# First projection on unscaled transposes, the row scale applied after the product

## The chip, the cores and the metric

The kernel runs on one core of a Trainium2 chip. The metric is the device time of one execution in microseconds (us); of several executions the median is given. Engines are named as in the profile: PE (TensorE, matrix products), DVE (VectorE), ACT (ScalarE), POOL (GpSimd), SP (SyncE, which issues most transfers).

## What is computed

Two transformer blocks on 256 rows of 2048 numbers, in float32. The change is in the first lines of the first block: a root-mean-square norm, and the projection `w_pw1` of a convolution module, whose output goes through a gate.

```python
def rms_norm(x, g):
    xf = x.astype(jnp.float32)
    y = xf * lax.rsqrt(jnp.mean(xf * xf, axis=-1, keepdims=True) + NORM_EPS)
    return (y * g.astype(jnp.float32)).astype(x.dtype)
...
def conformer_conv(h, w_pw1, b_pw1, w_dw, b_dw, ln_g, ln_b, w_pw2, b_pw2):
    u = h @ w_pw1 + b_pw1
    a, gate = jnp.split(u, 2, axis=-1)
    u = a * jax.nn.sigmoid(gate)
```

Behind it come a depthwise convolution over 31 rows, a layer norm, the projection `w_pw2`, a feed-forward part, and the second block with attention and another feed-forward part.

## The kernel before

**Split products.** Every float32 operand of a large product is split in two: `hi` is the operand rounded to the type that PE takes in one pass (`fp32r`), `lo` is the rest. A product is the sum of three, hi by hi, hi by lo and lo by hi. The weights are split as they arrive: ACT casts `raw` to `hi` (L127), DVE or POOL subtracts to get `lo` (L128). The activations are split the same way by `split_act` (L177: ACT casts, DVE subtracts).

**Steps.** The work is a list of steps, each with one weight tile (`unit_std` and its kind) and a function that issues its products. `emit` walks the list: it loads three tiles ahead (`LOADS`) and splits one tile ahead in the first three steps and two ahead later. All instructions are issued in the order in which the Python code runs, and each engine works through its own in that order. So where a line stands in `split` or in a step's function sets what waits behind it.

**The first projection.** `w_pw1` is worked in groups of 256 + 256 output columns (the value and its gate). A group has four steps, one for each quarter of the 2048 inputs; I call the step of group g and quarter c *unit (g, c)*. A unit is 4 column blocks by 4 input blocks by 3 products, 48 instructions on PE (L523, L525, L526), with tokens along the free axis (256 of them). The activations are transposed for that: tile `xa` c holds quarter c, hi and lo, and all groups read the same four tiles.

**The start, before.** x is loaded in four transfers of 512 KB (L253), and ACT sums the squares of all of it, eight times 512 columns (`sumsq`, L208). From the sums comes r = 1/rms for each row (`rstd_of`, L195). Only then ACT and DVE scale x by r (`first_a`, L298 and L300), PE transposes the scaled rows (L303), DVE multiplies by the norm's gain (`first_b`, L312), and `split_act` makes `xa`. The first product (L523) comes behind that.

**Behind a group.** After the last quarter `glu` (L348) applies the gate: ACT a sigmoid (L354), DVE a product that lands in PSUM (L358), ACT a copy (L360). `diags` (L363) makes diagonal matrices of the filter on ACT (L372), and `conv` (L383) runs 3 of 31 taps on PE (L391, tile `ca`) and the rest on DVE (L399). The conv of group 0 stands on PE behind unit (1, 0).

POOL splits the weights from tile 5 on in this part of the program (the kind "p" and i > 4 in `split`), and between tiles 6 and 7 it makes constants (L319 to L329).

## Time and profile before

| | |
|---|---|
| median of 3 runs | 2189.69 us (2189.35 to 2191.28) |
| the profiled execution | 2189.95 us, of which the profile's span is 2188.2 us |
| PE busy | 2151.5 us (98%) |
| DVE busy | 1439.0 us (66%) |
| ACT busy | 959.2 us (44%) |
| POOL busy | 175.2 us (8%) |
| transfers | 395.41 MB at a mean of 181 GB/s |

A row of a timeline gives start, length, engine, line, operation, the tiles (written<-read), the shapes and how many instructions were merged; in brackets stands how long the engine had been idle before, and what ended that. A row of the table by windows gives for each engine the busy time, and then PE's granted clock (1.00 is full), the busy share of the DMA engines, and GB/s.

### The profile page before, as it was taken

The numbers are of one execution on the slowest core, as the hardware profiler recorded it, in microseconds if no ns is written. First come the engines' busy times: TensorE is split into PE (matmuls) and PEld (weight loads), VectorE is DVE, ScalarE is ACT, GpSimd is POOL, SyncE is SP. The second block draws the span as 40 slices with busy tenths as digits, with TensorE's granted clock in tenths as the row PEclk, the third lists the DMA queues.
The fourth block names the chain that finished last, engine by engine and source line by source line (L and its number), as shares of the span: only waits on it lengthen the run. The fifth ranks groups of instructions, "written<-read, shape, count | busy, mean of one in ns | idle before, by whom it ended". The sixth has DMA issues, their size and how long they took to land.

```text
span 2188.2 us, 27599 instructions
## 1 busy us (share of the span) xinstructions
PE 2151.5 (98%) x11521; PEld 1862.8 (85%) x11521; DVE 1439.0 (66%) x1648; ACT 959.2 (44%) x965; POOL 175.2 (8%) x88
## 2 busy tenths in 40 slices
PE   7999899999999999999999999999999999999998
PEld 6999778888888888888788888888888888888886
DVE  5997775656665666566866565676656665666656
ACT  6454454434333433343545454454333433343333
POOL 2887500000000000000000000000000000000000
PEclk9999999999999999999999999999999999999999
DMA  7555255555655565556544554555565556555653
GB/s 228 164 165 148 74 184 192 189 192 178 202 193 192 178 205 192 189 179 221 177 161 154 176 170 154 162 185 181 192 204 191 178 190 203 189 182 195 196 190 133
DMA packets 219613, 395.41 MB, mean 181 GB/s; under 512 B 8994, under 2 KB 46018, under 8 KB 219074
## 3 DMA queue, kind: packets, MB, share of 16 engines
q1 hardware_dynamic: 216160, 389.05, 54.3%
q10 hardware_dynamic: 2960, 4.27, 0.6%
q8 instruction: 90, 1.47, 0.3%
q0 software_dynamic: 368, 0.34, 0.1%
q14 instruction: 35, 0.28, 0.0%
HBM read 391.53 MB, written 2.10 MB: 180 GB/s over the span
## 4 chain that ended last, share of the span: by engine, by line
PE 95%; DVE 2%; ACT 1%; issue 0%; DMA 0%; ACTq 0%; SPq 0%; DVEq 0%
PE up L219 21%; PE up L225 11%; PE dn L236 11%; PE dn L238 11%; PE dn L237 11%; PE pj L219 5%; PE pw L526 2%; PE pw L523 2%; PE pw L525 2%; PE pj L225 2%; PE ca L391 2%; PE wo L238 1%; PE wo L237 1%; PE wo L236 1%; PE pv L238 1%; PE pv L237 1%
## 5 line engine op out<-in xcount | busy, mean ns | idle before, releaser
L128 DVE TENSOR_TENSOR lo<-raw,hi 128x2048 fp32r<-128x2048 f32 (+1 forms) x339 | 774.3, 2284 | 511.1 <-ACT hi L127 510.8
L127 ACT CAST hi<-raw 128x2048 fp32r<-128x2048 f32 (+1 forms) x369 | 702.8, 1906 | 852.7 <-PE dn L238 320.1
L219 PE MATMUL up<-xn,hi 128*128 128x512 f32 x2048 | 482.3, 390 | 0.0
L219 PEld LDWEIGHTS up<-xn,hi 128*128 128x128 f32 x2048 | 380.2, 188 | 76.1
L236 PE MATMUL dn<-hi,act 128*128 128x512 f32 x1024 | 398.6, 389 | 0.0
L238 PE MATMUL dn<-hi,act 128*128 128x512 f32 x1024 | 398.4, 389 | 0.0
L237 PE MATMUL dn<-lo,act 128*128 128x512 f32 x1024 | 398.3, 389 | 0.0
L225 PEld LDWEIGHTS up<-xn,lo 128*128 128x128 f32 x2048 | 254.2, 192 | 5.0
L225 PE MATMUL up<-xn,lo 128*128 128x256 f32 x2048 | 255.7, 283 | 0.0
L646 DVE SCALAR_TENSOR_TENSOR res<-dn,rsq,res 128x512 f32<-128x512 f32 x256 | 191.3, 747 | 56.8 <-PE dn L238 56.8
L238 PEld LDWEIGHTS dn<-hi,act 128*128 128x128 f32 x1024 | 192.2, 188 | 40.0
L236 PEld LDWEIGHTS dn<-hi,act 128*128 128x128 f32 x1024 | 192.2, 188 | 39.8
L237 PEld LDWEIGHTS dn<-lo,act 128*128 128x128 f32 x1024 | 192.2, 188 | 39.8
L399 DVE SCALAR_TENSOR_TENSOR acc<-u_p,wd,acc 128x256 f32<-128x256 f32 x385 | 151.6, 474 | 0.0
L128 POOL TENSOR_TENSOR lo<-raw,hi 128x2048 fp32r<-128x2048 f32 x30 | 138.5, 4621 | 85.9 <-ACT hi L127 85.9
L523 PE MATMUL pw<-xa,hi 128*128 128x256 f32 x448 | 129.1, 288 | 0.7 <-ACT hi L127 0.7
L526 PE MATMUL pw<-xa,lo 128*128 128x256 f32 x448 | 127.6, 285 | 0.9 <-DVE lo L128 0.9
L525 PE MATMUL pw<-xa,hi 128*128 128x256 f32 x448 | 127.5, 285 | 0.0
L219 PE MATMUL pj<-xn,hi 128*128 128x512 f32 x512 | 122.4, 392 | 1.9 <-DVE q_t L911 1.9
L219 PEld LDWEIGHTS pj<-xn,hi 128*128 128x128 f32 x512 | 94.5, 188 | 21.8 <-DVE q_t L911 3.0
L631 ACT COPY u_t<-up 128x512 f32<-128x512 f32 x64 | 37.7, 589 | 159.6 <-PE up L219 159.6
L633 DVE TENSOR_TENSOR u_z<-up,u_t 128x512 f32<-128x512 f32 x64 | 44.3, 692 | 77.7 <-ACT u_t L631 77.7
(255 smaller groups left out, 2003.9 us busy)
## 6 DMA issues: line engine op xcount, KB each, us to landing
raw<-in_ffn_w_up_dram SPq DMA_DIRECT2D x64, 1024.0 KB, 5.1
raw<-in_ffn_w_down_dram SPq DMA_DIRECT2D x64, 1024.0 KB, 5.1
raw<-in_w_up_dram SPq DMA_DIRECT2D x64, 1024.0 KB, 5.1
raw<-in_w_down_dram SPq DMA_DIRECT2D x64, 1024.0 KB, 5.1
raw<-in_w_in_dram SPq DMA_DIRECT2D x48, 1024.0 KB, 5.0
raw<-in_conv_w_pw_dram SPq DMA_DIRECT2D x64, 512.0 KB, 4.8
raw<-in_conv_w_pw_dram SPq DMA_DIRECT2D x16, 1024.0 KB, 5.1
raw<-in_w_out_dram SPq DMA_DIRECT2D x16, 1024.0 KB, 5.0
```

Source lines behind the costliest of these rows:

```text
L127: nc.scalar.copy(hi[:, j:j + n], raw[:, j:j + n])
L128: e.tensor_tensor(out=lo[:, j:j + n], in0=raw[:, j:j + n], in1=hi[:, j:j + n].bitcast(F32), op=ALU.subtract)
L219: mm(ps[m], hi[:, k, m * P:(m + 1) * P], xt[:, k, :, :], start=(kq == 0 and k == 0), stop=(kq == 3 and k == 3), skip_group_check=True)
L225: mm(ps[m][:, 0:T], lo[:, k, m * P:(m + 1) * P], xt[:, k, 0, :], start=False, stop=False, skip_group_check=True)
L236: mm(ps[h], xh, hi[:, k, :], start=(first and k == 0), stop=False)
L237: mm(ps[h], xh, lo[:, k, :], start=False, stop=False)
L238: mm(ps[h], xl, hi[:, k, :], start=False, stop=(last and k == 3))
L399: nc.vector.scalar_tensor_tensor(out=acc[k], in0=src, scalar=w, in1=acc[k], op0=ALU.mult, op1=ALU.add)
L523: mm(ps[:, m, :], wh, xt[:, k, 0, :], start=first and m % 2 == 0, stop=False, skip_group_check=True)
L525: mm(ps[:, m, :], wh, xt[:, k, 1, :], start=False, stop=False, skip_group_check=True)
L526: mm(ps[:, m, :], wl, xt[:, k, 0, :], start=False, stop=last, skip_group_check=True)
L646: nc.vector.scalar_tensor_tensor(out=r, in0=ps[h], scalar=state["rsq"][:, h:h + 1], in1=r, op0=ALU.mult, op1=ALU.add)
```

## The change

It has five parts.

1. **Loads.** x now comes in eight transfers, by quarters of its columns, and the first three weight tiles are issued between the quarters. Weight tile 0 comes in four transfers (its two input halves apart) in place of two.
2. **Transposes of raw x.** `first_chunk` transposes x itself, not x times r. DVE's product with the gain writes to `xs_t` (a tile that the convolution needs later), and `split_act` splits from there. The first 32 products of unit (0, 0) (the two with `hi`) are issued in `first_products`, inside the split of tile 0; its 16 products with `lo` follow in the step. 14 transposes of the identity (`warm`) stand first on PE.
3. **The sums of squares** move from ACT's start into the splits of tiles 0 to 3, two for each. Where i > 0 they stand ahead of the cast of that tile.
4. **The scale after the product.** When all sums are there (behind the split of tile 3), `row_scales` makes r and two diagonal matrices of it; behind unit (0, 2) PE multiplies these by a matrix of ones, which spreads r along the tokens for every partition (`spread_scales`), and ACT copies that to `delta`. Group 0's result is multiplied by `delta` in PSUM ahead of its gate, two DVE instructions of 512 columns.
5. **The rescaled activations.** The other groups read `xa` too, so all four quarters in `xs_t` are multiplied by `delta` (`scale_chunk`: quarters 0 and 1 on DVE, 2 and 3 on POOL) and split again (`split_chunk`: ACT casts, and DVE or POOL subtracts): quarters 0 and 1 ahead of the splits of weight tiles 4 and 5, quarters 2 and 3 behind the gate and the diagonals of group 0, which move there too. The `lo` of weight tile 5 moves from POOL to DVE.

```diff
@@ split
         if i < 4:
-            for c in ((0, 1), (), (2,), (3,))[i]:
-                first_a(c)
-            first_b(i)
+            first_chunk(i)
+        elif i < 6:
+            split_chunk(i - 4)
+        if 0 < i < 4:
+            for h in range(2):
+                sumsq(state["ss0"], h, i)
...
-        e = nc.gpsimd if eng == "p" and i > 4 else nc.vector
+        e = nc.gpsimd if eng == "p" and i > 5 else nc.vector
...
+        if i == 0:
+            first_products(hi)
+            for h in range(2):
+                sumsq(state["ss0"], h, i)
+        if i == 3:
+            row_scales()
@@ prologue
+        for c in range(4):
+            for h in range(2):
+                nc.sync.dma_start(out=res[:, h, c * 512:(c + 1) * 512], in_=x[h * P:(h + 1) * P, c * 512:(c + 1) * 512])
+            if c < 3:
+                load(c)
+        at["load"] = 3
...
+        warm(14)
@@ new functions
+    def warm(n):
+        pt = ps1([P, 4, P], "warm")
+        for k in range(n):
+            nc.tensor.transpose(pt[:, k % 4, :], ident, ident)
+    def first_chunk(c):
...
+            for k in range(4):
+                nc.tensor.transpose(pt[:, k, :], res[:, h, (4 * c + k) * P:(4 * c + k + 1) * P], ident)
+            nc.vector.tensor_tensor(out=xs_t[:, 4 * c:4 * c + 4, h * P:(h + 1) * P], in0=pt, in1=g, op=ALU.mult)
+        for h in range(2):
+            tok = slice(h * P, (h + 1) * P)
+            split_act(xs_t[:, 4 * c:4 * c + 4, tok], xt[:, :, 0, tok], xt[:, :, 1, tok])
+    def row_scales():
+        r = rstd_of(state["ss0"], EPS1, "r0")
+        nc.scalar.preload_act_table_set("sigmoid_and_others")
+        dgr = state["dgr"] = wk([P, 2, P], "dgr")
+        for h in range(2):
+            nc.vector.tensor_scalar(out=dgr[:, h, :], in0=ident, scalar1=r[:, h:h + 1], scalar2=None, op0=ALU.mult)
+    def spread_scales():
+        dgr, pr = state.pop("dgr"), ps1([P, T], "pr0")
+        for h in range(2):
+            mm(pr[:, h * P:(h + 1) * P], ones, dgr[:, h, :], start=True, stop=True)
+        nc.scalar.copy(delta, pr)
+    def scale_chunk(c):
+        e, v = (nc.vector if c < 2 else nc.gpsimd), xs_t[:, 4 * c:4 * c + 4, :]
+        e.tensor_tensor(out=v, in0=v, in1=delta.unsqueeze(1).to_broadcast([P, 4, T]), op=ALU.mult)
+    def split_chunk(c):
+        e, v, xt = (nc.vector if c < 2 else nc.gpsimd), xs_t[:, 4 * c:4 * c + 4, :], state["xa"][c]
+        nc.scalar.copy(xt[:, :, 0, :], v)
+        e.tensor_tensor(out=xt[:, :, 1, :], in0=v, in1=xt[:, :, 0, :].bitcast(F32), op=ALU.subtract)
@@ glu
+        if gi == 0:
+            for m in (2, 0):
+                v = ps[:, m:m + 2, :]
+                nc.vector.tensor_tensor(out=v, in0=v, in1=delta.unsqueeze(1).to_broadcast([P, 2, T]), op=ALU.mult)
@@ the step of a group
+                    if gi == 0 and kq == 2:
+                        spread_scales()
+                        for c in range(4):
+                            scale_chunk(c)
                     if kq == 3:
                         glu(gi, ps)
+                        if gi == 0:
+                            state["dg", gi] = diags(gi)
+                            split_chunk(2)
+                            split_chunk(3)
```

Three places show how the order on the engines changes. (A number directly behind a name is the tile's index, the one behind the underscore only tells buffers apart.)

ACT between the first two weight tiles, before: quarter 1 of the activations is cast, then weight tile 1, and x times r for quarter 2.

```order
L127 CAST hi0_211<-raw0_166 128x1024 x2
L178 CAST xa1_155<-xf_220 128x4x128
L178 CAST xa1_155<-xf_222 128x4x128
L127 CAST hi1_228<-raw1_169 128x2048
L298 ACTIVATE xn_284<-res_83,r0_146 128x512
```

The same place now:

```order
L131 CAST hi0_186<-raw0_107 128x1024 x2
L218 ACTIVATE junk_225,ss0_142<-res_83 128x512
L218 ACTIVATE junk_227,ss0_142<-res_83 128x512
L188 CAST xa1_144<-xs_t_90 128x4x128 x2
L218 ACTIVATE junk_248,ss0_142<-res_83 128x512
L218 ACTIVATE junk_250,ss0_142<-res_83 128x512
L131 CAST hi1_252<-raw1_114 128x2048
```

Two sums of squares now stand between the cast of the activations and the cast of the weights; the quarters 2 and 3 have the same order.

DVE between the last weight tile of group 0 and the gate of group 0, before: constants, weight tile 4, the gate.

```order
L128 TENSOR_TENSOR lo3_384<-raw3_217,hi3_383 128x2048
L284 COPY vt_80<-pv_390 128x160
L290 COPY wd_81<-pw_394 128x8x31
L290 COPY wd_81<-pw_404 128x8x31
L128 TENSOR_TENSOR lo4_463<-raw4_232,hi4_462 128x2048
L356 MEMSET u_p_534 128x15
L664 TENSOR_TENSOR gcomb_82<-vt_80 128x16
L357 MEMSET u_p_534 128x15
L358 SCALAR_TENSOR_TENSOR u_p_534<-pw1_0_235,vt_80,sg_532 128x256
```

The same place now, from the constants on:

```order
L297 COPY wd_81<-pw_405 128x8x31
L342 TENSOR_TENSOR xs_t_90<-xs_t_90,delta_96 128x1024 x2
L714 TENSOR_TENSOR gcomb_82<-vt_80 128x16
L347 TENSOR_TENSOR xa0_143<-xs_t_90,xa0_143 128x4x256
L132 TENSOR_TENSOR lo4_474<-raw4_256,hi4_473 128x2048
L347 TENSOR_TENSOR xa1_144<-xs_t_90,xa1_144 128x4x256
L132 TENSOR_TENSOR lo5_483<-raw5_299,hi5_482 128x2048
L387 TENSOR_TENSOR pw1_0_192<-pw1_0_192,delta_96 128x512 x2
L392 MEMSET u_p_541 128x15
L393 MEMSET u_p_541 128x15
L394 SCALAR_TENSOR_TENSOR u_p_541<-pw1_0_192,vt_80,sg_539 128x256
```

The two scalings, the two splits of activations, weight tile 5 and the scaling of PSUM all stand ahead of the gate's product.

POOL at its first tensor operations, before:

```order
L128 TENSOR_TENSOR lo5_470<-raw5_310,hi5_469 128x2048
L128 TENSOR_TENSOR lo6_547<-raw6_387,hi6_546 128x2048
L319 MEMSET ones_c_75 128x128
L320 MEMSET fmask_76 128x384
L321 MEMSET smask_77 128x384
```

And now:

```order
L342 TENSOR_TENSOR xs_t_90<-xs_t_90,delta_96 128x1024 x2
L347 TENSOR_TENSOR xa2_145<-xs_t_90,xa2_145 128x4x256
L347 TENSOR_TENSOR xa3_146<-xs_t_90,xa3_146 128x4x256
L132 TENSOR_TENSOR lo6_566<-raw6_388,hi6_565 128x2048
L351 MEMSET ones_c_75 128x128
```

Four operations on the activations stand ahead of weight tile 6, and tile 5 is gone.

More of the change, by code (lines that the diff above doesn't have):

```diff
@@ L105, in load @@
         raw = wpool.tile([P, D], F32, tag="raw", name=f"raw{i}")
-        for k, width, off, ap in srcs:
-            dst = raw.rearrange("p (k c) -> p k c", k=k)
-            n = ap.shape[1]
-            nc.sync.dma_start(out=dst[:, :, off:off + n], in_=ap.rearrange("(k p) c -> p k c", p=P))
+        for q in range(1 if i else 2):
+            for k, width, off, ap in srcs:
+                dst = raw.rearrange("p (k c) -> p k c", k=k)
+                n, ks = ap.shape[1], slice(0, k) if i else slice(q * k // 2, (q + 1) * k // 2)
+                nc.sync.dma_start(out=dst[:, ks, off:off + n], in_=ap.rearrange("(k p) c -> p k c", p=P)[:, ks, :])
         raws[i] = raw
@@ L250, in prologue @@
         nc.scalar.preload_act_table_set(LOG_EXP)
-        for h in range(2):
-            for j in range(2):
-                nc.sync.dma_start(out=res[:, h, j * 1024:(j + 1) * 1024],
-                                  in_=x[h * P:(h + 1) * P, j * 1024:(j + 1) * 1024])
+        for c in range(4):
[4 more added lines that the diff above has]
+        at["load"] = 3
         make_identity(nc, ident)
@@ L266, in prologue @@
         state["raw_vectors"] = va, vb, wdr
-        ss0 = new_ss("ss0")
-        for h in range(2):
-            for j in range(2):
-                for c in range(2):
-                    sumsq(ss0, h, 2 * j + c)
-        r = rstd_of(ss0, EPS1, "r0")
-        state["r0"], state["xa"] = r, [xt_tile(f"xa{c}") for c in range(4)]
+        state["ss0"], state["xa"] = new_ss("ss0"), [xt_tile(f"xa{c}") for c in range(4)]
+        warm(14)
         pm = ps1([P, 16], "pm")
@@ L301, in first_a @@
+    def first_chunk(c):
+        g = vt[:, G_MIX + 4 * c:G_MIX + 4 * c + 4].unsqueeze(2).to_broadcast([P, 4, P])
+        xt = state["xa"][c]
+        for h in range(2):
             pt = ps1([P, 4, P], f"pt{h}{c}")
             for k in range(4):
[L303 to L315 removed]
+                nc.tensor.transpose(pt[:, k, :], res[:, h, (4 * c + k) * P:(4 * c + k + 1) * P], ident)
[3 more added lines that the diff above has]
+            split_act(xs_t[:, 4 * c:4 * c + 4, tok], xt[:, :, 0, tok], xt[:, :, 1, tok])
@@ new lines, in first_products @@
+    def first_products(hi):
+        ps = state["pw1"] = ps2([P, 4, T], "pw1_0")
+        for k in range(4):
+            for m in range(4):
+                for j in range(2):
+                    mm(ps[:, m, :], hi[:, k * 512 + m * P:k * 512 + (m + 1) * P], state["xa"][0][:, k, j, :],
+                       start=k == 0 and m % 2 == 0 and j == 0, stop=False, skip_group_check=True)
+    def row_scales():
[4 more added lines that the diff above has]
+            nc.vector.tensor_scalar(out=dgr[:, h, :], in0=ident, scalar1=r[:, h:h + 1], scalar2=None, op0=ALU.mult)
@@ L508, in fn @@
                 def fn(hi, lo, kq=kq):
-                    if kq == 0:
+                    if kq == 0 and gi > 0:
                         state["pw1"] = ps2([P, 4, T], f"pw1_{gi}")
@@ L512, in fn @@
                         vectors()
-                    if kq == (3 if gi == 0 else 0):
+                    if kq == 0 and gi > 0:
                         state["dg", gi] = diags(gi)
@@ L517, in fn @@
                     ps, xt = state["pw1"], state["xa"][kq]
+                    if gi == 0 and kq == 0:
+                        for k in range(4):
+                            for m in range(4):
+                                mm(ps[:, m, :], lo[:, k, m * P:(m + 1) * P], xt[:, k, 0, :], start=False, stop=False,
+                                   skip_group_check=True)
+                        return
                     for m in range(4):
```

20 lines of the change are left out of this document (removed).

## The prediction

> **What bounds the kernel now.** I read the page first, then PE's busy time by windows, then the timelines of the first 75 us and the chain of waits.
>
> ```profile
> span 2188.2 us, 27599 instructions
> PE 2151.5 (98%) x11521; PEld 1862.8 (85%) x11521; DVE 1439.0 (66%) x1648; ACT 959.2 (44%) x965; POOL 175.2 (8%) x88
> ```
> ```profile
> 0.00:20.00 20.00, 4.97 (x23) 4.29 (x24) 6.36 (x19) 11.93 (x25) 7.89 (x21) 1.00 0.90 279
> 20.00:40.00 20.00, 19.82 (x157) 19.18 (x156) 15.59 (x18) 12.14 (x12) 0.00 (x0) 0.91 0.50 158
> 40.00:60.00 20.00, 20.00 (x159) 19.68 (x158) 14.00 (x36) 11.91 (x20) 11.61 (x12) 1.00 0.69 225
> 60.00:80.00 20.00, 20.00 (x166) 19.92 (x165) 18.78 (x52) 9.05 (x14) 15.42 (x4) 1.00 0.60 198
> ```
>
> PE is the bound from 20 us on: 20.00 of 20 us in the third and fourth window. The start costs 15 us of idle PE, and that is all the change can win; whatever it makes PE wait for later is lost one for one, since no slack follows. So the sum is that of one moment: when unit (1, 3), the last of group 1, ends.
>
> ```profile
> 27.79 0.36 PE L523 MATMUL pw<-xa,hi 128*128 128x256 f32 x1
> 42.06 0.28 PE L523 MATMUL pw<-xa,hi 128*128 128x256 f32 x1
> 53.74 2.59 PE ca L391 x12
> 73.65 0.47 ACT L354 ACTIVATE sg<-pw,vt 128x256 f32<-128x256 f32 x1 [3.93 <-PE pw L526]
> ```
>
> Before, unit (0, 1) starts at 27.8, unit (0, 3) at 42.1, the first convolution on PE at 53.7, and group 1 ends at 73.6, where its sigmoid is released. These are the marks.
>
> **Part 1 and 2: when the first products start.**
>
> ```profile
> 1.08 0.29 POOL masks.py:199 TENSOR_SCALAR_AFFINE_SELECT ident<-ident 128x128 f32<-128x128 f32 x1
> 5.16 0.63 ACT L208 ACTIVATE junk<-res 128x512 f32<-128x512 f32 x1 [3.08 <-DMA res<-in_x_dram]
> 5.92 0.63 ACT L208 ACTIVATE junk<-res 128x512 f32<-128x512 f32 x1
> 13.79 3.67 PE L303 MATMUL pt<-ident,xn 128*128 128x128 f32 x16 [9.07 <-ACT xn L298]
> 14.94 0.69 DVE L312 TENSOR_TENSOR xf<-pt,vt 128x512 f32<-128x512 f32 x1 [1.04 <-PE pt L303]
> 15.67 0.62 ACT L178 CAST xa<-xf 128x512 fp32r<-128x512 f32 x1 [1.32 <-DVE xf L312]
> 17.11 1.99 ACT L127 CAST hi<-raw 128x1024 fp32r<-128x1024 f32 x2
> 19.69 0.28 PE L523 MATMUL pw<-xa,hi 128*128 128x256 f32 x1
> 19.81 0.28 PE L525 MATMUL pw<-xa,hi 128*128 128x256 f32 x1
> 21.00:22.00 1.00, 1.00 (x6) 1.00 (x6) 0.91 (x3) 0.82 (x2) 0.00 (x0) 0.50 0.28 45
> 21.18 0.41 PE L526 MATMUL pw<-xa,lo 128*128 128x256 f32 x1
> 21.39 0.41 PE L523 MATMUL pw<-xa,hi 128*128 128x256 f32 x1
> ```
>
> The identity is ready at 1.08 + 0.29 = 1.4; 14 transposes at 3.67/16 = 0.23 end at 4.6, on an idle PE, so they cost nothing. The first 512 KB of x released ACT at 5.16, and now they are quarter 0. Its last four transposes end at 5.2 + 4 x 0.23 = 6.1; gain 0.69, cast 0.62, half of weight tile 0 (1.99/2 = 1.0): 8.4. Products start at 8.5. The smaller transfers carry the same bytes: 279 GB/s bring the 3.0 MB up to weight tile 1 in 11 us, ahead of its cast below.
>
> The 32 products stand 0.12 us apart at full clock (19.69 to 19.81) and 0.21 at half (21.18 to 21.39, where the granted clock is 0.50). That is 3.8 or 6.7 us; I take the middle, 5.3, since the idle 2 us before them can bring the half clock back: they end at 13.8. Eight transposes at full clock (half of 1.8, 0.9): 14.7.
>
> Whether the transposes raise the clock is open in one place. Before, sixteen of them ran 0.23 apart until 17.5, and the products behind them ran 0.12 apart, so here they did. The Trainium skill (TensorE: Matmul & The Clock Gate, Part 4) says that transposes don't count as busy for the clock gate; by it the first products would all take 0.21 and the sum would grow by 6.7 - 5.3 = 1.4 us. The rows disagree with it, so I don't take it.
>
> **Part 3: the head start shrinks.**
>
> ```profile
> 22.30 1.89 ACT L127 CAST hi<-raw 128x2048 fp32r<-128x2048 f32 x1
> 24.23 2.29 DVE L128 TENSOR_TENSOR lo<-raw,hi 128x2048 fp32r<-128x2048 f32 x1 [1.10 <-ACT hi L127]
> 11.56 0.16 DVE L199 TENSOR_REDUCE rs_a<-ss 128x2 f32<-128x8 f32 x1 [10.54 <-ACT junk L208]
> 12.82 0.16 DVE L193 SCALAR_TENSOR_TENSOR r<-rs_t,r 128x2 f32<-128x2 f32 x1
> ```
>
> From a quarter's last transpose to its weights' `lo` everything is in a row: gain 0.69, cast 0.62, two sums of squares at 5.92 - 5.16 = 0.76 each (they stand ahead of the weights' cast), cast 1.89, subtraction 2.29, hand-overs 0.2: 7.2 us. For quarter 1 that is 14.7 + 7.2 = 21.9. PE has 16 products (1.9) and eight transposes (0.9) for these 7.2 us, and idles 4.4. Unit (0, 1) starts at 21.9, a head start of 5.9.
>
> An idle PE of that length starts at half clock: before, 17.5 to 20.6 was mostly idle and the clock fell to 0.50; the window 20 to 40 shows 0.91, so 0.09 x 20 / 0.5 = 3.6 us at half. Again 3.6 us at half cost 1.8: unit (0, 1) takes 48 x 0.12 + 1.8 = 7.6 and ends at 29.5, quarter 3's transposes at 30.4. DVE comes free by its own chain at 21.9 + 0.69 + 7.2 = 29.8, so PE sets it. Quarter 3: 30.4 + 7.2 = 37.6; r takes 12.82 + 0.16 - 11.56 = 1.4, the two diagonals 2 x 0.28: 39.5; PE spreads them in some 0.5 (two small float32 products, bounds 0.2 and 0.8). Unit (0, 3) starts at 40.0: a head start of 2.1. The table load (1.28 us) is over by then.
>
> ```profile
> L691 DVE TENSOR_SCALAR dgr<-ident,rt x2: 282/284/286, 1087.5 to 1087.7; 128x128 f32<-128x128 f32 x2
> ```
>
> **Part 4 and 5: the rescale, without port conflicts.**
>
> ```profile
> 268.37 0.68 DVE L179 TENSOR_TENSOR y<-xs_t,y 128x512 fp32r<-128x512 f32 x1
> 44.00 1.86 ACT L372 ACTIVATE dg<-ident,wd 128x128 f32<-128x128 f32 x6
> 48.53 0.49 DVE L358 SCALAR_TENSOR_TENSOR u_p<-pw,vt,sg 128x256 f32<-128x256 f32 x1 [4.83 <-ACT sg L354]
> 49.44 0.37 ACT L360 COPY u<-u_p 128x256 f32<-128x256 f32 x1 [0.94 <-DVE u_p L357]
> 53.00 4.59 POOL L128 TENSOR_TENSOR lo<-raw,hi 128x2048 fp32r<-128x2048 f32 x1 [4.22 <-ACT hi L127]
> 57.53 0.21 POOL L319 MEMSET ones_c<- 128x128 f32 x1
> 59.79 4.66 POOL L128 TENSOR_TENSOR lo<-raw,hi 128x2048 fp32r<-128x2048 f32 x1
> ```
>
> A DVE operation on 1024 columns I take as half of 2.29, 1.2 (two of 512 would be 1.36); POOL's as half of 4.59, 2.3. `delta` is copied at 40.4. DVE: two scalings to 42.8, `gcomb` 43.0, split of quarter 0 44.2; ACT: cast of quarter 0 at 42.6, weight tile 4 at 44.5; DVE: its `lo` 46.8 (unit (0, 3) ended at 45.8, so PE waits 1 us), quarter 1 48.0, tile 5 50.3, PSUM twice 0.69 51.7. The gate (0.3 for the margins, 0.49, 0.37, sigmoid 0.47, 0.49, 0.37, hand-overs) ends at 54.4, the diagonals (1.86) at 56.3; PE, done with unit (1, 0) at 52.4, has waited, and the convolution ends at 56.9, against 53.74 + 2.59 = 56.3 before: the head start is gone. Behind the diagonals ACT casts quarter 2 (57.3), POOL splits quarters 2 and 3 (61.9), then weight tile 6 (66.5), the constants (59.79 - 57.53 = 2.3) and tile 7 (4.6): 73.4. PE ends unit (1, 1) at 62.7, waits 3.8 for tile 6, ends unit (1, 2) at 72.0, waits 1.4 for tile 7, and ends group 1 46 products later, at 78.9. Before: 73.6. Without conflicts the change loses **5.3 us**.
>
> **What POOL and DVE do to each other.**
>
> ```profile
> 269.96 4.77 POOL L128 TENSOR_TENSOR lo<-raw,hi 128x2048 fp32r<-128x2048 f32 x1 [9.37 <-ACT hi L127]
> 271.57 3.72 DVE L179 TENSOR_TENSOR y<-xs_t,y 128x512 fp32r<-128x512 f32 x1 [1.31 <-ACT y L178]
> ```
>
> A DVE subtraction of two SBUF tiles that takes 0.68 took 3.72 when it met POOL's: it ended at 275.29, 0.56 after POOL's end at 274.73, so it stood still until then. In the change POOL's two scalings (4.6) are released by the same copy of `delta` as DVE's row of two-input operations. If they take turns, DVE's scalings end at 41.6 and 45.1, POOL's at 43.9 and 47.4, quarter 0 at 48.8, tile 4 at 51.1 in place of 46.8: 4.3 us later, and all behind it too. If DVE's queued operations keep their turn, POOL gets in only at DVE's first gap, ahead of tile 4: 2.2 later. No row shows two waiting queues; bounds 0 and 4.6, and I take 4.3, nearest to the row. The Trainium skill (SBUF — State Buffer, Who interferes with whom) says that the one which issues first holds the shared ports for its whole instruction; it doesn't say who is next. With it the sum is at 2.2 or 4.3, without it at 0.
>
> With PE idle for 5 us ahead of unit (1, 0) and 4 ahead of (1, 2), the second half clock (1.8) mostly falls where PE waits for POOL anyway; 0.4 is left. Sum: 5.3 + 4.3 + 0.4 = **10.0 us slower**: 2199.95 by the profiled execution (2189.95, its span and 1.75 around it), and from the median 2189.69 + 10.0 = **2199.7**.
>
> **The rivals.**
> - *The head start is kept* (the other side). If everything from the spread to weight tile 6 fits behind PE's own work (three units and the convolution, 3 x 5.76 + 2.6 = 19.9 us), PE never waits and what is won stays: 2.1 as at unit (0, 3), up to the 5.9 of unit (0, 1) if quarters 2 and 3 lose nothing either; in the middle 4.0, 2185.7. For it: PE is dense there before. Against: the chain is 66.5 - 40.0 = 26.5 us, or 30.8 with turns; it breaks even only if tile 7 is done at 68.1, 5.3 us earlier. Chance 0.07.
> - *No conflict and a warm clock.* The ports don't clash and the warm-up holds: 3.8 us for the first products (1.5 less), and in unit (0, 1) no half clock, so DVE's chain ends last, at 29.8 in place of 30.4 (0.6 less): 5.3 - 2.1 = 3.2 slower, 2192.9. For it: the transposes raised the clock before. Against: the row of 3.72. Chance 0.13.
> - *Half the conflict.* No conflict with a cold clock (5.3, 2195.0) or DVE keeping its turn (5.3 + 2.2 + 0.4 = 7.9, 2197.6). Chance 0.25.
> - *Colder and longer.* Half clock in all first products (1.4) and another 3.6 us of it where PE doesn't wait (1.8): 13.2, 2202.9. Chance 0.10.
> - *The forecast*, turns with one cold stretch: 2199.7, chance 0.45.
>
> **How the numbers follow.** The range goes from 2192.5 to 2203.0: it leaves out the kept head start (0.07) and the outer part of the coldest case. A difference of 0.2% (4.4 us) is about what a measurement of this kernel can tell. Slower by more: forecast, half the conflict and colder, 0.45 + 0.25 + 0.10 = 0.80. Within: 0.13, from the second rival, and 0.03 of the first (gains up to 4.4), 0.16. Faster: the rest of the first, 0.04.
>
> **What would show it.** Right: the first product at 8 to 9 us; ACT's sums of squares directly ahead of the weight casts and PE idle for some 4 us ahead of unit (0, 1), which starts near 22; the spread near 40; DVE's operations at L342 or L347 longer than 1.2 us while POOL runs L342; PE waiting ahead of the first convolution and, for POOL's L132, ahead of unit (1, 2); group 1's sigmoid near 83. Wrong: PE dense from 40 to 75 (first rival), DVE's operations of 1.2 us beside POOL's (second or third), or a difference that arises behind 90 us, for which nothing here gives a reason.

## The result and the profile after

The changed kernel takes 2201.32 us (median, 2201.12 to 2202.75, 6 runs) against 2189.93 us of the kernel before on the same chip (2189.35 to 2191.28, 6 runs): a ratio of 1.0051, 95% interval 1.0041 to 1.0061. It is slower by 11.4 us, where 10.0 were forecast. The profiled execution took 2201.44 us, of which 2199.7 are its span. One execution among the experiments (3611.93 us at a granted clock of 0.56, of the kernel without the rescale, whose other nine took 2187.76 to 2189.52) was in a slower state and no difference is read from it.

The page's first lines, and the table by windows (PE, PEld, DVE, ACT, POOL, then PE's granted clock, DMA share, GB/s):

```profile
span 2199.7 us, 27650 instructions
PE 2160.2 (98%) x11539; PEld 1870.4 (85%) x11539; DVE 1450.3 (66%) x1653; ACT 960.3 (44%) x966; POOL 182.0 (8%) x91
```
```profile
0.00:20.00 20.00, 15.30 (x87) 14.30 (x87) 8.08 (x16) 9.07 (x16) 7.91 (x21) 1.00 0.92 284
20.00:40.00 20.00, 15.97 (x122) 15.31 (x122) 12.68 (x16) 10.79 (x18) 0.00 (x0) 0.91 0.48 156
40.00:60.00 20.00, 14.42 (x101) 13.86 (x102) 18.39 (x23) 9.00 (x13) 6.76 (x2) 0.91 0.49 156
60.00:80.00 20.00, 17.08 (x120) 16.57 (x119) 20.00 (x52) 11.47 (x16) 17.91 (x14) 0.91 0.33 110
80.00:100.00 20.00, 20.00 (x160) 19.67 (x159) 16.09 (x45) 9.00 (x14) 18.03 (x6) 1.00 0.65 208
```

PE is busy 10 us more in the first 20 us than before (3.3 us of it are the warm-up), and then has holes in the three windows in which it was dense; from 80 us on it is dense again. So the loss arises ahead of 85 us. PE's timeline gives the places (start, length, and in brackets the idle time and what ended it), with the sigmoid of group 1 on ACT as the last row:

```profile
1.43 3.25 PE L303 MATMUL warm<-ident 128*128 128x128 f32 x14 [1.43 <-POOL ident masks.py:199]
4.83 1.97 PE L312 MATMUL pt<-ident,res 128*128 128x128 f32 x8
9.18 6.28 PE L323 MATMUL pw<-xa,hi 128*128 128x256 f32 x32 [2.38 <-ACT hi L131]
15.29 1.04 PE L312 MATMUL pt<-ident,res 128*128 128x128 f32 x8
...
23.42 0.39 PE L568 MATMUL pw<-xa,lo 128*128 128x256 f32 x1 [1.82 <-DVE lo L132]
...
40.47 0.68 PE L337 MATMUL pr<-dgr,ones 128*128 128x128 f32 x4 [1.58 <-DVE dgr L332]
40.91 0.36 PE L565 MATMUL pw<-xa,hi 128*128 128x256 f32 x1
...
49.63 0.39 PE L567 MATMUL pw<-xa,hi 128*128 128x256 f32 x1 [2.62 <-DVE xa L347]
51.84 0.58 PE L568 MATMUL pw<-xa,lo 128*128 128x256 f32 x1 [1.81 <-DVE lo L132]
...
59.72 2.83 PE L427 MATMUL ca<-u,dg 128*128 128x256 f32 x12 [0.68 <-issue]
71.46 0.39 PE L568 MATMUL pw<-xa,lo 128*128 128x256 f32 x1 [2.92 <-POOL lo L132]
```
```profile
84.53 0.48 ACT L390 ACTIVATE sg<-pw,vt 128x256 f32<-128x256 f32 x1 [3.92 <-PE pw L568]
```

The marks of the prediction beside this (a row's start, or start plus length):

| mark (us) | before | forecast | after |
|---|---|---|---|
| unit (0, 1) runs | 27.8 | 21.9 | 23.4 |
| spread of r | none | 39.5 | 40.5 |
| unit (0, 3) starts | 42.1 | 40.0 | 40.9 |
| `lo` of tile 4 ready | 43.5 | 51.1 | 51.8 |
| group 1's sigmoid | 73.65 | 83.6 | 84.5 |

The change is 4.4 us ahead at unit (0, 1), 1.2 ahead at unit (0, 3), and 10.9 behind at the end of group 1. Of the waits behind unit (0, 3), DVE ends the two ahead of the convolution and POOL the last. What DVE and POOL did from the copy of `delta` on (DVE's rows, then POOL's):

```profile
41.59 4.58 DVE L342 TENSOR_TENSOR xs_t<-xs_t,delta 128x1024 f32<-128x1024 f32 x2 [0.20 <-ACT delta L338]
46.10 2.34 DVE L714 TENSOR_TENSOR gcomb<-vt 128x16 f32<-128x16 f32 x1
48.37 1.21 DVE L347 TENSOR_TENSOR xa<-xs_t,xa 128x1024 fp32r<-128x1024 f32 x1
49.50 2.28 DVE L132 TENSOR_TENSOR lo<-raw,hi 128x2048 fp32r<-128x2048 f32 x1
```
```profile
41.65 6.76 POOL L342 TENSOR_TENSOR xs_t<-xs_t,delta 128x1024 f32<-128x1024 f32 x2 [31.88 <-ACT delta L338]
62.09 4.79 POOL L347 TENSOR_TENSOR xa<-xs_t,xa 128x1024 fp32r<-128x1024 f32 x2 [13.68 <-ACT xa L346]
66.84 4.57 POOL L132 TENSOR_TENSOR lo<-raw,hi 128x2048 fp32r<-128x2048 f32 x1
```

Two scalings on DVE take 4.58 us in place of 2.4, two on POOL 6.76 in place of 4.6, and the product `gcomb` of 128 x 16 takes 2.34. One by one, DVE's first scaling ends at 42.82, POOL's first at 45.09, DVE's second at 46.17, POOL's second at 48.41 and `gcomb` at 48.44: each engine stands until the other's running operation ends, in turns. Behind that POOL idles 13.7 us, until ACT casts quarter 2 behind the gate; it splits quarters 2 and 3 in 4.79 us, and only then begins tile 6, at 66.84.

Ahead of it, ACT's rows for quarter 1 show the sums of squares between the cast of the activations and that of the weights:

```profile
16.66 1.22 ACT L188 CAST xa<-xs_t 128x512 fp32r<-128x512 f32 x2 [5.21 <-DVE xs_t L313]
17.78 0.62 ACT L218 ACTIVATE junk<-res 128x512 f32<-128x512 f32 x1
...
18.53 0.63 ACT L218 ACTIVATE junk<-res 128x512 f32<-128x512 f32 x1
...
19.16 1.88 ACT L131 CAST hi<-raw 128x2048 fp32r<-128x2048 f32 x1
```

### The profile page after: what moved, and what is told of

Read it like the earlier page. It is cut to its first block, busy times and chain, and to the rows that moved or that the text cites. A ratio compares the mean times of both kernels' runs of the same rounds, so it can differ in the third digit from the quotient of the medians.

```text
span 2199.7 us, 27650 instructions
## 1 busy us (share of the span) xinstructions
PE 2160.2 (98%) x11539; PEld 1870.4 (85%) x11539; DVE 1450.3 (66%) x1653; ACT 960.3 (44%) x966; POOL 182.0 (8%) x91
## 4 chain that ended last, share of the span: by engine, by line
PE 93%; DVE 2%; issue 2%; ACT 1%; DMA 1%; POOL 1%; SPq 0%; ACTq 0%; DVEq 0%; POOLq 0%
PE up L229 21%; PE up L235 11%; PE dn L248 11%; PE dn L247 11%; PE dn L246 11%; PE pj L229 5%; PE pj L235 2%; PE pw L568 2%; PE pw L567 2%; PE pw L565 2%; PE ca L427 2%; PE wo L248 1%; PE wo L247 1%; PE wo L246 1%; PE pv L248 1%
## 5 line engine op out<-in xcount | busy, mean ns | idle before, releaser
L132 DVE TENSOR_TENSOR lo<-raw,hi 128x2048 fp32r<-128x2048 f32 (+1 forms) x340 | 776.4, 2284 | 515.7 <-ACT hi L131 512.5
L132 POOL TENSOR_TENSOR lo<-raw,hi 128x2048 fp32r<-128x2048 f32 x29 | 133.8, 4619 | 46.0 <-ACT hi L131 46.0
L565 PE MATMUL pw<-xa,hi 128*128 128x256 f32 x432 | 125.9, 291 | 2.0 <-ACT hi L131 2.0
L567 PE MATMUL pw<-xa,hi 128*128 128x256 f32 x432 | 124.4, 288 | 2.6 <-DVE xa L347 2.6
```

Of the source, the lines that this page charges most:

```text
L132: e.tensor_tensor(out=lo[:, j:j + n], in0=raw[:, j:j + n], in1=hi[:, j:j + n].bitcast(F32), op=ALU.subtract)
L565: mm(ps[:, m, :], wh, xt[:, k, 0, :], start=first and m % 2 == 0, stop=False, skip_group_check=True)
L567: mm(ps[:, m, :], wh, xt[:, k, 1, :], start=False, stop=False, skip_group_check=True)
```

## The experiments

The theory was the prediction's: the sums of squares in the cast's way, turns of POOL and DVE, a start at half clock, and a rescale that ends later than PE's own work. The rivals were a delay that is hidden anyway and a rescale too large for DVE and POOL in any order. Each edit is to the changed kernel. Every kernel ran beside the kernel before on one chip, and its ratio to that stands with it (the kernel before had medians of 2189.79 to 2190.87 there); differences in us are to the changed kernel's median, 2201.32, so a us of them is within what chips and executions differ by. Two things in the traces say how far a difference of 1 to 2 us can be read. The same start brought the spread of r at 39.21 to 40.84 us in five executions. And in four profiled executions (POOL's scalings later, the factor from PSUM, the bridge, no warm-up) the granted clock is 0.91 in the window 290 to 310, where the others have 1.00; with POOL's scalings later the lag behind the kernel before grows there from 5.9 to 7.6 us, although the edit lies over 200 us ahead. So the place of group 1's sigmoid is given beside the times.

### POOL's scalings later

POOL's two scalings wait for ACT's first sigmoid of group 0 (a copy of `delta` made there), when DVE's row is done.

```diff
-        e.tensor_tensor(out=v, in0=v, in1=delta.unsqueeze(1).to_broadcast([P, 4, T]), op=ALU.mult)
+        e.tensor_tensor(out=v, in0=v, in1=(delta if c < 2 else lnr).unsqueeze(1).to_broadcast([P, 4, T]), op=ALU.mult)
...
+            if gi == 0 and i == 0:
+                nc.scalar.copy(lnr, delta)
+                scale_chunk(2)
+                scale_chunk(3)
...
-                        for c in range(4):
+                        for c in range(2):
                             scale_chunk(c)
```

> POOL's two scalings read a second copy of the row scale that ACT makes behind the first sigmoid of group 0, when DVE has no more operations with two SBUF inputs; no work is left out. Turn theory (DVE and POOL take turns at a shared port): DVE's second scaling and gcomb fall from 3.4 and 2.3 us to 1.2 and 0.2, quarter 0 is split 4.3 us earlier, and some 4 us of the loss come back: 2197 us (2196 to 2198.5). Work theory (the engines only have more to do, in whatever order): DVE's operations keep their lengths or POOL's later start costs what DVE wins: 2200.5 to 2203. Clock theory (PE's half clock is the loss): no change, 2201.

Measured: 2197.53 us (2196.82 to 2198.12), ratio 1.0034 (1.0021 to 1.0047). DVE's row in its timeline:

```profile
40.34 2.36 DVE L342 TENSOR_TENSOR xs_t<-xs_t,delta 128x1024 f32<-128x1024 f32 x2 [0.20 <-ACT delta L338]
42.62 0.17 DVE L718 TENSOR_TENSOR gcomb<-vt 128x16 f32<-128x16 f32 x1
42.70 1.22 DVE L347 TENSOR_TENSOR xa<-xs_t,xa 128x1024 fp32r<-128x1024 f32 x1
44.49 2.29 DVE L132 TENSOR_TENSOR lo<-raw,hi 128x2048 fp32r<-128x2048 f32 x1 [0.57 <-ACT hi L131]
```

The scalings take 2.36 us, `gcomb` 0.17. From the scalings' start to tile 4's `lo` it is 44.49 + 2.29 - 40.34 = 6.4 us, against 49.50 + 2.28 - 41.59 = 10.2 with turns: 3.8 us. The time fell by 3.8, or by 4.5 when each kernel is taken against the kernel before on its own chip, so the price in time is 4 us to within 1. From the spread to group 1's sigmoid (39.21 to 79.57) it is 40.4 us, against 40.47 to 84.53, 44.1, in the changed kernel: 3.7 less. The turns are shown, with their price.

### One DVE instruction out of the row

Only `gcomb` moves, ahead of the scalings, behind the copy of the constants.

```diff
         nc.vector.tensor_copy(vt[:, 0:160], pv[:, 0:160])
+        nc.vector.tensor_tensor(out=gcomb, in0=vt[:, G_FIN:G_FIN + 16], in1=vt[:, G_ATTN:G_ATTN + 16], op=ALU.mult)
```

> The changed kernel with one DVE instruction moved: the product gcomb of 128 x 16, which took 2.34 us between DVE's scalings and the split of quarter 0, now stands behind the copy of the constants, ahead of the scalings. Theory that the engines alternate whatever the size of an operation: the split of quarter 0 takes gcomb's place and waits for POOL's second scaling in its stead, 3.4 us long, and ends at 49.6 as before: 2201.3 us (2200.4 to 2202.2). Rival: the small operation lost the turn for all behind it, and without it quarter 0 is split 2.2 us earlier: 2199.1.

Measured: 2200.42 us (2200.29 to 2201.91), ratio 1.0048 (1.0032 to 1.0063). DVE's row:

```profile
40.66 4.59 DVE L343 TENSOR_TENSOR xs_t<-xs_t,delta 128x1024 f32<-128x1024 f32 x2
45.17 3.39 DVE L348 TENSOR_TENSOR xa<-xs_t,xa 128x1024 fp32r<-128x1024 f32 x1
```

The split of quarter 0 takes over the wait, 3.39 us in place of 1.21. It ends 45.17 + 3.39 - 40.66 = 7.9 us behind the scalings' start; in the changed kernel it was 48.37 + 1.21 - 41.59 = 8.0. Whatever DVE operation of two SBUF tiles is next has the wait. From the spread (39.53) to group 1's sigmoid (83.50) it is 44.0 us, as in the changed kernel; the 0.9 us in the time lie ahead of the spread, where nothing was changed.

### The factor from PSUM

DVE's scalings read r from the PSUM tile that the spread wrote, so only one input is in SBUF.

```diff
+        state["pr0"] = pr
...
-        e.tensor_tensor(out=v, in0=v, in1=delta.unsqueeze(1).to_broadcast([P, 4, T]), op=ALU.mult)
+        e.tensor_tensor(out=v, in0=v, in1=(state["pr0"] if c < 2 else delta).unsqueeze(1).to_broadcast([P, 4, T]), op=ALU.mult)
```

> DVE's two scalings read the factor from PSUM (the tile that the spread wrote), so they have one SBUF input; POOL's stay as they are. Theory that the engines take turns only where both DVE inputs are in SBUF: DVE's scalings take 1.2 us each beside POOL's first, POOL's 2.3 each; DVE's next operation (gcomb, or the split of quarter 0) then still waits for POOL's second one and ends near 46.4 in place of 48.4; weight tile 4 comes 1.9 us earlier and group 1 ends that much earlier: 2199.4 us (2198.3 to 2200.5). Rival: any DVE operation on SBUF data waits for POOL's, so the scalings again take 3.4 us: 2201.3. Second rival: the delay is not where the time goes, scalings short but the total unchanged: 2201.3 with L342 at 1.2 us.

Measured: 2198.65 us (2197.23 to 2200.43), ratio 1.0038 (1.0024 to 1.0051). DVE's row, then POOL's:

```profile
41.96 2.35 DVE L343 TENSOR_TENSOR xs_t<-xs_t,pr 128x1024 f32<-128x1024 f32 x2 [0.20 <-ACT delta L338]
44.30 1.23 DVE L348 TENSOR_TENSOR xa<-xs_t,xa 128x1024 fp32r<-128x1024 f32 x1
45.45 2.39 DVE L715 TENSOR_TENSOR gcomb<-vt 128x16 f32<-128x16 f32 x1
47.76 2.28 DVE L132 TENSOR_TENSOR lo<-raw,hi 128x2048 fp32r<-128x2048 f32 x1
```
```profile
42.01 5.79 POOL L343 TENSOR_TENSOR xs_t<-xs_t,delta 128x1024 f32<-128x1024 f32 x2 [32.15 <-ACT delta L338]
```

Two scalings beside POOL's first take 2.35 us, as alone. The expected order behind them was wrong in one point: the split of quarter 0 won its turn (1.23 us), POOL's second scaling waited for it, and `gcomb` then waited for POOL. Tile 4's `lo` comes 8.1 us behind the scalings' start in place of 10.2, and from the spread (40.84) to group 1's sigmoid (82.38) it is 41.5 us in place of 44.1. The Trainium skill (SBUF — State Buffer, Who interferes with whom) says that a DVE instruction with two SBUF inputs contends with POOL's reads, that one with at most one, outside its 2-port modes, does not, and that order of issue and not the shape decides who blocks; the trace agrees, with 2.35 against 4.58 us for the scalings and 2.34 against 0.17 for `gcomb`.

### Sums of squares behind the weights' cast

```diff
-        if 0 < i < 4:
-            for h in range(2):
-                sumsq(state["ss0"], h, i)
         raw = raws.pop(i)
...
         if i == 0:
             first_products(hi)
+        if i < 4:
             for h in range(2):
                 sumsq(state["ss0"], h, i)
```

> The sums of squares of quarters 1 to 3 stand behind the cast of the weight tile on ACT in place of ahead of it; no work is left out. Chain theory (activations, sums, cast, subtraction stand in a row): each of the quarters' chains is up to 1.5 us shorter, the spread of the row scale comes at 37.5 to 38 us in place of 40.5, and group 1 ends some 2.5 us earlier: 2198.8 us (2197.8 to 2200). Clock or work theory: ACT is idle enough that the order doesn't matter, 2200.8 to 2201.8.

Measured: 2198.14 us (2195.95 to 2201.42), ratio 1.0043 (1.0026 to 1.006); 3.2 us less by the medians, though its runs are 5.5 us apart. Where PE spreads r, in the profiled execution (2195.95 us, the fastest):

```profile
35.55 0.68 PE L335 MATMUL pr<-dgr,ones 128*128 128x128 f32 x4 [0.22 <-DVE dgr L330]
```

The spread stands at 35.55 in place of 40.47 and is hardly waited for, and group 1's sigmoid at 79.18, 5.4 earlier. Against the 39.21 to 40.84 of the same start in five executions that is 3.7 to 5.3 us, so this trace shows that the sums' place delays the spread. In time the size is open: two of the four executions took 2195.95 and 2196.13 us, the other two 2200.16 and 2201.42, hardly less than the changed kernel.

### A gap-free start, and none at all

Ten more transposes of the identity between the transposes of quarter 0 and the first products:

```diff
             first_chunk(i)
+            if i == 0:
+                warm(10)
```

> Ten more transposes of the identity between the transposes of quarter 0 and the first products, where PE idles 2.4 us; nothing is left out. If transposes count for PE's clock when they leave no gap, the clock is full by 7.3 or 10.7 us, the 32 first products take 3.9 to 5 us in place of 6.1, and the chain behind them is 1 to 2 us earlier: 2199.8 us (2199 to 2200.5). If transposes don't count: the first products stay 0.21 us apart until about 14 us, 2201.3 (2200.8 to 2201.8).

Measured: 2199.49 us (2198.87 to 2200.43), ratio 1.0044 (1.003 to 1.0059), 1.8 us less. And without the 14 at the start (`warm(14)` removed):

> The changed kernel without the 14 transposes of the identity at the start. In the changed kernel the granted clock was at half until 14.1 us in spite of them, so by the theory that only a gap-free stretch of transposes raises the clock they do nothing: 2201.3 us (2200.5 to 2202.1), the first products again 0.21 us apart at their start and near 0.12 at their end. Rival: they do bring the clock to full some us earlier than it would come without them, so that all first products and unit (0, 1) lie at half: 2.5 us more, 2203.8. In either case the first product starts at 9.2 us, because its weights' cast releases it.

Measured: 2201.91 us (2200.58 to 2202.27), ratio 1.0051 (1.0037 to 1.0065). The first products, with the bridge and without the warm-up:

```profile
9.18 4.10 PE L325 MATMUL pw<-xa,hi 128*128 128x256 f32 x32 [1.00 <-ACT hi L133]
```
```profile
8.50 5.83 PE L322 MATMUL pw<-xa,hi 128*128 128x256 f32 x32 [2.38 <-ACT hi L131]
```

32 products take 4.10 us with the bridge, 6.28 in the changed kernel, 5.83 without the warm-up. At full clock, 0.12 us apart, they would take 31 x 0.12 + 0.28 = 4.0. Over all profiles the two groups do not overlap: with the bridge the 32 products take 4.09 or 4.10 us (four kernels, 1.0 to 1.45 us of idle PE ahead of them), with the change's start 5.58 to 6.72 (six kernels, 2.38 to 2.61 us idle). So transposes do raise the clock when little idle time stands behind them, and the 14 of the change, with 2.4 us of idle PE before the products, do nothing that can be measured in time. They are not free either: without them the transposes of x start at 3.93 in place of 4.83. How the clock is lost shows in the kernel with the factor from PSUM, whose start is that of the changed kernel:

```profile
4.59 1.22 PE L312 MATMUL pt<-ident,res 128*128 128x128 f32 x8
8.42 6.72 PE L323 MATMUL pw<-xa,hi 128*128 128x256 f32 x32 [2.61 <-ACT hi L131]
```

There the eight transposes of x ran at full clock behind the warm-up (1.22 us), and the products behind 2.61 us of idle PE still ran at half (6.72). In the changed kernel's own execution the clock had not risen by then: its transposes took 1.97. The bridge adds transposes and shortens the idle time at once; but where the eight transposes already ran at full clock, the products took 5.58 and 6.72 us behind the longer idle time (POOL's scalings later, factor from PSUM) and 4.09 or 4.10 behind the shorter one (the three kernels below that have the bridge too), which points to the idle time and not to their number. The Trainium skill (TensorE: Matmul & The Clock Gate, Part 4) says that transposes don't count as busy for the gate; the rows of 4.10 and 1.22 us disagree, since nothing but transposes ran ahead of them. The granted clock in the windows' rows is 1.00 for the first 20 us in both kernels, because the trace holds no change of the clock ahead of its first record: at the very start the clock is read from how far apart the products stand.

### The rescale left out

The scalings and second splits of the activations are left out; the other groups read unscaled activations.

```diff
-        elif i < 6:
-            split_chunk(i - 4)
...
-                        for c in range(4):
-                            scale_chunk(c)
...
-                            split_chunk(2)
-                            split_chunk(3)
```

> The rescaled activations are left out (no scaling and no second split of the four quarters; the other groups read the unscaled activations). All else of the change stays, the scaling of group 0 in PSUM and weight tile 5 on DVE too. Chain theory: behind the spread PE never waits long, the head start of 1 us at unit (0, 3) is about what is left, less what the gate behind tile 5 costs: 2189.5 us (2188 to 2191), so that the rescale is the whole loss. Clock theory: the early half clock stays, 2195 or more.

Measured: 2189.35 us, ratio 0.9994 (0.9984 to 1.0003). The same kernel once more, for where its time goes:

> The same kernel as in the fourth experiment (the scalings and second splits of the activations left out, the other groups read unscaled activations), for its profile. If the rescale is all that costs later, PE has no wait for L347 or for POOL's L132 behind unit (0, 3), and what the early start won stays: group 1's sigmoid at 71.5 to 73.5 (before 73.65), 2188 to 2190 us. Rival: the multiplication in PSUM and the diagonals behind the gate cost a wait of their own ahead of the first convolution, 1 to 3 us, and eat the rest of the head start: sigmoid at 74 to 76, and 2190 to 2192 us.

Measured: 2189.61 us. The window 40 to 60, and group 1's sigmoid:

```profile
40.00:60.00 20.00, 19.50 (x153) 19.20 (x154) 16.64 (x37) 13.37 (x22) 4.24 (x1) 1.00 0.62 211
```
```profile
73.13 0.47 ACT L388 ACTIVATE sg<-pw,vt 128x256 f32<-128x256 f32 x1 [4.40 <-PE pw L566]
```

PE is dense, and the sigmoid stands at 73.13, 11.4 us earlier than with the rescale. Behind the spread PE has no wait of over 0.3 us, so the multiplication in PSUM and the diagonals behind the gate cost none to speak of. But 73.13 is only 0.5 ahead of before: this start, with its sums of squares and half clock, has next to nothing to give even where the rescale is free.

### The three edits together

> The changed kernel with the three edits of the earlier experiments together: POOL's scalings behind the first sigmoid, the sums of squares behind the weight casts, ten more transposes between the first transposes and the first products. If the three costs add, 3.8 + 3.2 + 1.8 = 8.8 us are saved: 2192.5. I expect somewhat less, since POOL's row (its scalings, quarters 2 and 3, weight tile 6, constants, weight tile 7) is late in all three and ends last then: 2194 (2192.3 to 2195.8), group 1's sigmoid at 76 to 78.5. Rival: one cost hides the other two (PE waits for the same tile whatever comes earlier): 2197, no better than the first edit alone.

Measured: 2192.78 us (2191.97 to 2194.8), ratio 1.0013 (1.0004 to 1.0022). That is 8.5 us less than the changed kernel, where the single edits sum to 3.8 + 3.2 + 1.8 = 8.8. Against the kernel before on each chip it is 8.4, and the single edits are 4.5 + 3.8 + 2.5 = 10.8; so no cost hides the other two, but that they add in full isn't shown. Group 1's sigmoid is at 75.13, earlier than expected. In the trace the turns come back whole (40.3 us from the spread to the sigmoid, as with POOL's scalings later alone), while the spread, at 34.83, is 5.6 us earlier where the two single edits had 4.9 and 2.3.

### Rearranged

Besides the bridge, the late sums and the factor from PSUM: diagonals and the splits of quarters 2 and 3 ahead of group 0's gate, the splits of quarter 1 and of tile 5 behind it (`late5`), POOL's constants at the start.

```diff
...
                     if kq == 3:
-                        glu(gi, ps)
                         if gi == 0:
                             state["dg", gi] = diags(gi)
                             split_chunk(2)
                             split_chunk(3)
+                        glu(gi, ps)
+                        if gi == 0:
+                            state.pop("late5")()
```

> The changed kernel rearranged so that nothing of its new work should stand ahead of what PE needs next: sums of squares behind the weight casts; ten more transposes ahead of the first products; DVE's scalings read the factor from PSUM; the diagonals and the splits of quarters 2 and 3 ahead of group 0's gate; the split of quarter 1 and of weight tile 5 behind that gate; POOL's constants at the kernel's start. Theory (the change loses by the place of its new work, not by its amount): PE is dense from unit (0, 3) at 36 us on but for 1 to 3 us, group 1's sigmoid at 69 to 72 against 73.65 in the kernel before: 2186.5 us (2185 to 2189), ratio to the kernel before 0.9982. Rival: the added work itself (four scalings, four splits, two multiplications in PSUM) doesn't fit on DVE and POOL between 36 and 62 us in any order: 2192 or more.

Measured: 2188.76 us (2186.89 to 2191.99), ratio 0.9995 (0.9986 to 1.0004): not to be told from the kernel before. Its sigmoid and the one wait of over 2 us that is left ahead of it:

```profile
42.77 0.58 PE L577 MATMUL pw<-xa,lo 128*128 128x256 f32 x1 [2.58 <-DVE lo L132]
```
```profile
69.72 0.47 ACT L399 ACTIVATE sg<-pw,vt 128x256 f32<-128x256 f32 x1 [3.92 <-PE pw L577]
```

It is 73.65 - 69.72 = 3.9 us ahead at the end of group 1. The profiled execution, at 2186.89 the fastest, kept 3.0 of it (the span is 2185.2 against 2188.2); the medians show 1.0. In the profiled execution 0.6 is given back close behind, at the convolution of group 1, which waits for ACT's copy (the kernel before first, then this one):

```profile
79.21 2.75 PE L391 MATMUL ca<-u,dg 128*128 128x256 f32 x12
```
```profile
75.89 2.87 PE L436 MATMUL ca<-u,dg 128*128 128x256 f32 x12 [0.45 <-ACT u L405]
```

It is 3.3 us ahead there, and still 3.2 at the first product behind the layer norm (262.11 against 265.30). What the other executions lost is open; only one was profiled.

The last kernel moves what that trace showed: DVE scales quarters 0 to 2 from PSUM and POOL only quarter 3; tile 4 is split ahead of quarter 0; `gcomb` early; the casts of quarter 1 and tile 5 ahead of the gate.

```diff
...
                     if gi == 0 and kq == 2:
                         spread_scales()
-                        for c in range(4):
+                        for c in (0, 1, 3):
                             scale_chunk(c)
                     if kq == 3:
-                        glu(gi, ps)
                         if gi == 0:
+                            scale_chunk(2)
                             state["dg", gi] = diags(gi)
-                            split_chunk(2)
-                            split_chunk(3)
+                            cast_chunk(1)
+                            state.pop("cast5")(0)
+                            cast_chunk(3)
+                            rest_chunk(3)
+                        glu(gi, ps)
+                        if gi == 0:
+                            cast_chunk(2)
+                            rest_chunk(1)
+                            state.pop("rest5")(0)
+                            rest_chunk(2)
```

> The rearranged kernel (e8) with what its trace still showed in PE's way moved too: POOL scales only quarter 3, DVE scales quarters 0 to 2 from PSUM, quarter 2 after the subtraction of weight tile 4; the cast and subtraction of weight tile 4 stand ahead of quarter 0's; the small product gcomb moves ahead of the scalings; the casts of quarter 1 and of weight tile 5 stand ahead of group 0's gate. Theory (order and turns are all that is lost, no resource is full): no DVE operation meets POOL's before 43 us, unit (1, 0) starts at 40.5 in place of 42.8, (1, 1) at 50 in place of 52.05, group 1 ends near 67.5, and no half clock near 42: 2185.5 us (2184 to 2187.5), ratio 0.998. Rival: POOL's quarters 2 and 3 and weight tile 6 end last in this order too: PE waits 2 us ahead of unit (1, 2) and the time is that of e8, 2188.8.

Measured: 2185.64 us (2184.32 to 2186.37), ratio 0.9977 (0.9967 to 0.9986): 5.2 us less than the kernel before on the same chip (2190.84), and 15.7 less than the changed kernel. The window 40 to 60, DVE beside POOL, and the sigmoid:

```profile
40.00:60.00 20.00, 19.07 (x148) 18.34 (x147) 18.80 (x41) 12.97 (x17) 15.40 (x4) 1.00 0.63 205
```
```profile
34.99 2.35 DVE L365 TENSOR_TENSOR xs_t<-xs_t,pr 128x1024 f32<-128x1024 f32 x2
37.26 2.37 DVE L131 TENSOR_TENSOR lo<-raw,hi 128x2048 fp32r<-128x2048 f32 x1
```
```profile
67.40 0.47 ACT L403 ACTIVATE sg<-pw,vt 128x256 f32<-128x256 f32 x1 [3.93 <-PE pw L581]
```

DVE does as much as in the changed kernel in this window (18.80 us against 18.39) and POOL more, and PE is dense at full clock: 6.3 us are won at the end of group 1. The rival, that the added work is too large for any order, falls.

The marks of the profiled executions side by side (us):

| kernel | spread of r | group 1's sigmoid | between |
|---|---|---|---|
| changed | 40.47 | 84.53 | 44.1 |
| POOL's scalings later | 39.21 | 79.57 | 40.4 |
| `gcomb` out of the row | 39.53 | 83.50 | 44.0 |
| factor from PSUM | 40.84 | 82.38 | 41.5 |
| sums behind the cast | 35.55 | 79.18 | 43.6 |
| bridge | 38.14 | 82.03 | 43.9 |
| no warm-up | 39.37 | 83.45 | 44.1 |
| three edits together | 34.83 | 75.13 | 40.3 |
| rearranged | 33.52 | 69.72 | 36.2 |
| last | 33.86 | 67.40 | 33.5 |
| rescale left out | 40.50 | 73.13 | 32.6 |

The edits to the start move the spread, those to the turns and the order shorten what lies behind it. Behind the spread the rescale costs 44.06 - 32.63 = 11.4 us in the order of the change, of which the turns are 3.7, and about 0.9 us in the last order. Of the 17.1 us that the last kernel's sigmoid is earlier than the changed kernel's, 6.6 lie ahead of the spread.

## Why the prediction was right, and where its sizes were off

**What bounds.** PE was the bound, and nothing was lost behind the start except 0.6 us: the spans differ by 2199.7 - 2188.2 = 11.5, the sigmoids by 10.9. The first product behind the layer norm is still 10.9 later (276.18 against 265.30), so the 0.6 arise behind it. No experiment took them up.

**When the first products start.** Forecast 8.5, measured 9.18. The forecast had four transposes of x left at 5.2 and done at 6.1; in fact all eight stood behind the warm-up, started at 4.83 and took 1.97 us, until 6.80, which is the 0.7 us. Where they ran at full clock (1.22, with the factor from PSUM) the first products started at 8.42. The 32 products, taken at the middle of 3.8 and 6.7 as 5.3, took 15.29 - 9.18 = 6.1: the mis-sized term of this step. The value should have come from the end at half clock, since the transposes were followed by 2.4 us of idle PE. The reason given for the middle, that the idle time can bring the half clock back, was sound; that the transposes would count was right too (4.10 us with the bridge), only not across the gap. That the warm-up costs nothing was not so for x's transposes, which start 0.9 us earlier without it.

**The shrinking head start.** 7.2 us from a quarter's last transpose to its weights' `lo` were forecast: 15.29 + 1.04 = 16.3 to the product released at 23.42 is 7.1. Unit (0, 1) was 1.5 us later than forecast, of which the two terms above are 0.7 + 0.8. Its half clock was there (0.91 in the window 20 to 40). The spread came at 40.5 where 39.5 was forecast, unit (0, 3) at 40.9 for 40.0. A head start of 2.1 was 1.2. That the sums' place is part of what shrinks it is shown by the spread at 35.55 without them in the way.

**The rescale and the turns.** The row of 3.72 us that the prediction took from the layer norm carried the right rule to another place: turns at 4.3 us were forecast, and 3.8 measured, by the trace and by the time of the kernel without them. The third turn fell on `gcomb`, which the prediction does not say (it names L342 and L347 as the ones that wait). The split of quarter 0 ended 8.0 us behind the start of the scalings, where 48.8 - 40.4 = 8.4 were forecast. The case that DVE keeps its turn (2.2) is ruled out by POOL's first scaling, which ended at 45.09, ahead of DVE's second at 46.17. The waits behind it came as listed: DVE ahead of unit (1, 0), the gate ahead of the convolution, POOL's `L132` ahead of unit (1, 2), 2.92 us for a forecast of 3.8. The wait for tile 7 did not come: unit (1, 2) ran part of its products at half clock (0.91 in the window 60 to 80) and took its place. Where the clock was full there, PE did wait for tile 7, 0.82 us with the sums behind the cast and 0.83 with the factor from PSUM.

**The sum.** From unit (0, 3) to group 1's sigmoid 84.53 - 40.91 = 43.6 us passed, and 73.65 - 42.06 = 31.6 before: 12.0 longer, for 83.6 - 40.0 = 43.6 forecast. The 0.9 us that the sigmoid was late came in ahead of unit (0, 3), from the first products. The two stretches, after and before:

```profile
40.91:84.53 43.62, 35.59 (x257) 34.49 (x256) 39.43 (x77) 20.43 (x28) 29.20 (x17) 0.92 0.43 142
```
```profile
42.06:73.65 31.59, 31.59 (x256) 31.27 (x255) 25.58 (x67) 15.73 (x23) 24.50 (x14) 1.00 0.69 232
```

That this step comes out to 0.1 us is luck. PE idled 43.6 - 35.6 = 8.0 us, where the waits of the prediction are some 12 (1 + 4.3 ahead of unit (1, 0), 56.9 - 2.6 - 52.4 = 1.9 ahead of the convolution, 3.8 for tile 6, 1.4 for tile 7): measured were 4.4, 0.7, 2.9 and none. In their place stands half clock: 0.08 x 43.6 / 0.5 = 7.0 us of it, which cost half of that, 3.5, where the prediction added 0.4. The prediction was right about which tiles PE waits for, and that half clock falls in the main where PE would wait anyway; the sizes of its terms were off on both sides and made up for each other.

**The rivals.** A kept head start needed everything behind PE's own work, which the order of the change excludes; with the order of the last kernel it came true (6.3 us at group 1's end). No conflict with a warm clock falls by 4.58 and 6.28 us, half the conflict by the measured turns. The colder case was nearer than its 0.10 says: the first products ran at half clock, and two more such stretches fell into the windows 40 to 60 and 60 to 80; the time stayed below its 2202.9, as the two fell where the forecast had waits.

## What to carry to other kernels

A start that is made shorter only moves the work that fed it: ask which engine does that work now, at what moment, and which tile of the next stage stands behind it in that engine's queue, since here nearly the same work cost 11.4 us in one order and won 5.2 in another. Price operations that DVE and POOL run at the same time on SBUF tiles from rows in which both are busy, and look for the operand that can come from PSUM. Fill the time between a warm-up and the first product: here it bought nothing until ten more transposes did that. When a sum comes out right, compare its terms with the trace too: here waits that were too long stood for half clock that was left out.

## What the runs showed of the hardware

- DVE and POOL took strict turns in the rows where both had queued operations of two SBUF tiles, whatever the size: `gcomb` of 128 x 16 took 2.34 us in its turn and 0.17 without it.
- A DVE operation with one input in PSUM runs at its own 1.2 us beside POOL's 2.4, but the next one of two SBUF tiles makes POOL's operation wait in turn: POOL's two took 5.79 us.
- Behind a warm-up of transposes, 32 products took 5.58 to 6.72 us in six executions where PE had idled 2.4 to 2.6 us ahead of them, and 4.09 or 4.10 in four where it had idled 1.0 to 1.45 us.
